# Feed-forward of an encoder layer on one core: stationary tiles in other addresses, a tanh one place later, three stretches in another order

## The chip, the cores and the metric

The kernel runs on one core of a Trainium2 chip. The metric is the device time of one execution in microseconds, less is better. PE is TensorE, DVE is VectorE, ACT is ScalarE, POOL is GpSimd and SP is SyncE, whose queue issues nearly all transfers.

## The reference

The part that matters is the last third of the layer, for 2048 tokens, width 1024 and a hidden width of 2816. All arithmetic is float32.

```python
hff = rms_norm(x, g_norm2) * (1.0 + scale2) + shift2
gte, up = jnp.split(hff @ w_ffn_in, 2, axis=-1)
ff = (jax.nn.silu(gte) * up) @ w_ffn_out
x = x + gate2 * ff            # then rms_norm(x, g_final)
```

## The kernel before, in words

**Arithmetic.** A float32 operand is split into a high and a low part (ACT copies the high part, DVE subtracts to get the low one), and each product is three matmuls: high by high, high by low, low by high (`mm3`, lines 56 to 58). Both large products of the feed-forward are done blockwise with seven block products in place of eight (A11, A12, S4, A22, S1, S2, S3), so that sums and differences of blocks have to be made on POOL and DVE.

**First product, units.** `pair(hh, j, ...)` is one unit: half `hh` of the tokens, block `j` of the hidden columns. It runs seven products on PE, `prod(0)` to `prod(6)`, of 12 matmuls each (four blocks of K, three matmuls each), 84 in all. The weights of a unit are the stationary operand, the activations (`hop`, seven operands of 128x4x512) the moving one. Products 0, 2, 4 and 6 add on in one PSUM bank (`ps1`): each waits until the sum before it has been copied out, by ACT in lines 1564 (`s1`), 1572 (`u2`) and 1578 (`u3`). Product 5 adds on in `ps5`, which ACT copies out in line 1575 (`c5`). Two tanh stand in a unit: line 1568 on `g0`, which DVE makes in line 1567 from product 1, and line 1583 on `u2`. Results are stored to DRAM (`a_d`) by `stores()`, at the head of the next unit. There are 44 units: 22 for the first half of the tokens, 22 for the second.

**Weights.** `load_raw` fetches the weights of a unit (three transfers, `graw`, `A21`, `A22r`), and `weights` makes the seven split tiles from them, in steps that `beside` hands out between the products of the unit before (`STEPS`). The split tiles come from a ring of 12 slots of 4 KB: `big28` to `big31`, the four tiles of pool `w`, and `r0` to `r3` in pool `ff`.

**The turn.** Unit 21 is the last of the first half of the tokens. There `refill_ops(1)` loads the seven `hop` operands of the second half in their old places, operand u as soon as product u of unit 21 is done (`start`), in two pieces of 512 KB each, and `finish_op` splits them on ACT and DVE (lines 1371, 1372). Units 21 and 22 use the same weights. The splits of operands 5 and 6 stand between the first products of unit 22.

**Second product, passes.** Seven passes (A11, S2, S3, A22, S1, S4, A12) go over 11 steps of K each. A step takes one stationary pair (`ah`, `al`, from `raw_a` and `split_a`) and one weight tile `w2`, 24 matmuls in eight PSUM banks. The stationary pairs come from a ring of four (`aring`): two pairs in `r0` to `r3`, two in pool `w`. The `w2` tiles lie in the four `xt` tiles of pool `xp`.

**Addresses.** Pools on the left side start at 0 and those on the right hang down from 224 KB of each partition. In the feed-forward the left side holds constants up to 5 KB, the 32 tiles of `big` up to 133 KB, pool `w` up to 155 KB and pool `xp` from there (its four `xt` from 155 to 171 KB). On the right is `ff`, 184 to 224 KB, with `r0` to `r3` at 200 to 216 KB.

**Order.** PE follows the program's order throughout. DVE, ACT, POOL and SP follow the order written in the program (a manual schedule, `rest`) up to `rest.close()`, which stands after the last unit. What is written behind it is put in order by the scheduler, which may also place it among the instructions of the region.

Of the kernel before, what the change touches and what calls it, by code (L numbers as in the profile page):

```python
# [21 lines left out]
P = 128  # L22
T = 2048
D = 1024
# [12 lines left out]
def hybrid_layer_kernel(  # L37
# [1276 lines left out]
    def norm2(hh, z, tags, lead):  # L1314
        n = BO[2 * hh + z]
        xt = [xp.tile([P, D], F32, tag="xt", name="x1t", bufs=4) for _ in range(4)]
# [42 lines left out]
    def refill_ops(hh):  # L1359
# [9 lines left out]
        def finish(u):  # L1369
            for hi, lo in zip(*hls[u]):  # L1370
# [6 lines left out]
                 + [("ff", f"r{i}") for i in range(4)])  # L1377
# [7 lines left out]
    def load_raw(j, early=False):  # L1385
# [4 lines left out]
        a22 = (xd.tile([P, 512], F32, tag="n2", name="A22r", bufs=9) if early else  # L1390
               pools["ff"].tile([P, 512], F32, tag="tm", name="A22r", bufs=2))
        cg, cu = (slice(o + j * P, o + (j + 1) * P) for o in (0, DFF))
        sp.dma_start(v(g), w_ffn_in[:, cg].rearrange("(k p) c -> p k c", p=P))
        sp.dma_start(v(a21), w_ffn_in[0:512, cu].rearrange("(k p) c -> p k c", p=P))
        sp.dma_start(v(a22), w_ffn_in[512:1024, cu].rearrange("(k p) c -> p k c", p=P))
        return g, a21, a22
# [38 lines left out]
    for p in range(NPR):  # L1435
# [4 lines left out]
        if p == NPR - 1:  # L1440
            hop, finish_op, refill = refill_ops(0)

            def after(u):
                if u == 6:
                    raws.append(load_raw(KH, True))
                refill(u)
                if u > 2:
                    finish_op(u - 3)
            first_w = weights(first_raw, True)
        fill.append(out_proj(cur, xr0, after))  # L1450
        for i in range(28):
# [12 lines left out]
            if i == 8 and p == NPR - 2:  # L1464
                first_raw = load_raw(0, True)
# [62 lines left out]
    with tc.tile_pool(name="ff", bufs=1, side="right", reuse_waits="tile") as ff:  # L1528
# [15 lines left out]
        def pair(hh, j, ws_, hop, after=lambda u: None, then=lambda u: None):  # L1544
# [23 lines left out]
            act.activation(t0, g0, AF.Tanh, scale=0.5)  # L1568
            dve.scalar_tensor_tensor(g0, t0, 1.0, g0, ADD, MUL)
            then(1)  # L1570
            prod(2, ps1)
            act.activation(u2, ps1, AF.Copy)  # L1572
            then(2)
# [45 lines left out]
        raw, = raws  # L1619
        for n, (hh, j) in enumerate(units[:-1]):  # L1620
# [5 lines left out]
            else:  # L1626
                more_w = weights(raw)
            STEPS = (0, 0, 0, 2, 2, 1, 2) if n == 0 else (0, 0, 1, 1, 2, 2, 1)

            def beside(u):  # L1630

                nonlocal nxt_w, raw
# [4 lines left out]
                if turn:  # L1637
                    if u > 1:
                        finish_op(u - 2)
                    return  # L1640
                for _ in range(STEPS[u]):
                    nxt_w = next(more_w)
                if u == 6 and wseq:
# [9 lines left out]
        aring = deque([("ff", f"r{i}") for i in range(4)] + [("w", f"w{i}{z}") for i in (1, 0) for z in "hl"])  # L1653
        wring = deque([("xp", "xt")] * 4)
# [73 lines left out]
        def operands(u, k):  # L1728
            if u == "A11":
                load_w2(W11, k)  # L1730
            if u == "S2":
                load_w2(W22, k)
            a = load_a(u, k)
            w = op_w(u, k)
            if u == "A11" :
                load_w2(W12, k)
            return a, w

        g2h = wp.tile([P, D], F32, tag="wraw", name="g2h", bufs=1)
        early, raw_ = [], []  # L1740

        def first_operands(u):

            if u < 2:
                raw_.append(raw_a("A11", u))
            if u == 2:
                sp.dma_start(g2h, gate_d[1].partition_broadcast(P))
            if u in (2, 4):
                early.append((split_a(*raw_[u // 2 - 1]), op_w("A11", u // 2 - 1)))
            if u in (3, 5):  # L1750
                load_w2(W12, u // 2 - 1)
            if u == 5:
                pool.tensor_scalar(g2h, g2h, 0.5, None, MUL)

        for k in range(2):
# [3 lines left out]
        rest.close()  # L1759
# [57 lines left out]
        def evac(u, i, ps):  # L1817
            if u == "A11":
                ra.append(big(16 + i, "ra", (P, D), F32))
            if u == "S3":  # L1820
                rb.append(big(24 + i, "rb", (P, D), F32))
# [21 lines left out]
        for u in ("A11", "S2", "S3", "A22", "S1", "S4", "A12"):  # L1843
# [56 lines left out]
```

## Time and profile before

| | |
|---|---|
| median of 3 runs | 2343.58 us (2342.69 to 2345.49) |
| the profiled execution | 2334.39 us |
| its span, first to last instruction | 2332.6 us |
| PE busy | 2247.8 us, 96% of the span, 10822 matmuls |
| DVE, ACT, POOL busy | 1609.4, 1062.4, 1047.1 us |
| mean granted clock of PE | 0.991 |
| units (first product) | 1013.9 to 1890.4 us of the span |
| passes (second product) | 1890.4 to 2324.4 us |

A row of the timeline is the start in the span, the duration, the engine, the line of the program, the operation with its tiles, and in brackets how long the engine had been idle and what ended that. Matmuls overlap in the pipeline, so a matmul's duration (0.39 us) is longer than the distance from one start to the next, and it is the distance that counts. A row that ends in x2 is two instructions one after the other.

### The profile page before, as it was taken

The page shows a single profiled execution, that of the slowest core. Times are in us where ns is not written, and L with a number is a line of the kernel's source. Part 1 is how long each engine was busy: PE and PEld are TensorE (multiplying, and loading weights), DVE is VectorE, ACT ScalarE, POOL GpSimd, SP SyncE. Part 2 cuts the span into 40 slices and gives each one's busy share as a digit, 9 for nine tenths or more (in the row PEclk, how much of TensorE's full clock was granted, in tenths as well). Part 3 has the DMA queues.
Part 4 walks back from the last instruction along what each step waited for, and adds up shares of the span by engine and source line. Part 5 has one row for each costly group of instructions (what it writes and reads, how often), then busy time and mean ns, then how long its engine had stood idle before and what let it go on. Part 6 is the DMA issues. An engine that isn't in the chain of part 4 may idle for free.

```text
span 2332.6 us, 32476 instructions
## 1 busy us (share of the span) xinstructions
PE 2247.8 (96%) x10822; PEld 1862.1 (80%) x10822; DVE 1609.4 (69%) x2995; ACT 1062.4 (46%) x2206; POOL 1047.1 (45%) x876
## 2 busy tenths in 40 slices
PE   7999989999999999999999999899999979999998
PEld 4997778888888878778888887688888868888887
DVE  6786667767687887786666776666666635685594
ACT  5424555544577756354444434333333323232352
POOL 1007534334334344536565655556565652592020
PEclk9999999999999999999999999999999999999999
DMA  8486755676766576764343445223232373543462
GB/s 331 150 256 218 241 155 163 176 215 188 200 176 191 169 245 218 256 221 144 109 167 104 162 159 201 83 95 109 95 108 95 127 261 100 159 153 100 136 217 90
DMA packets 355499, 393.38 MB, mean 169 GB/s; under 512 B 21388, under 2 KB 253180, under 8 KB 355332
## 3 DMA queue, kind: packets, MB, share of 16 engines
q1 hardware_dynamic: 355108, 391.28, 52.2%
q8 instruction: 85, 1.39, 0.2%
q14 instruction: 82, 0.67, 0.1%
q10 hardware_dynamic: 224, 0.04, 0.0%
HBM read 272.05 MB, written 119.19 MB: 168 GB/s over the span
## 4 chain that ended last, share of the span: by engine, by line
PE 54%; DVE 1%; DMA 1%; issue 1%; ACT 1%; POOL 0%; SPq 0%; DVEq 0%; ACTq 0%; POOLq 0%
PE fp L56 12%; PE fp L58 12%; PE fp L57 12%; PE fo L58 6%; PE fo L56 6%; PE fo L57 6%; PE ops L56 1%; DMA al<-a_d 1%; PE ops L58 1%; PE ops L57 1%; DMA B<-hop_d 0%; PE trn L166 0%; DVE B L1372 0%; DVE T L1372 0%; DMA T<-hop_d 0%
## 5 line engine op out<-in xcount | busy, mean ns | idle before, releaser
L466 PE MATMUL gps<-hT,whi 128*128 128x512 f32 x1088 | 397.3, 419 | 0.2 <-DVE cacc L500 0.2
L56 PE MATMUL fo<-w,ah 128*128 128x512 f32 x616 | 242.3, 393 | 5.0 <-ACT ah L1667 2.3
L58 PE MATMUL fo<-w,al 128*128 128x512 f32 x616 | 242.4, 393 | 1.2 <-DVE al L1668 1.2
L57 PE MATMUL fo<-w,ah 128*128 128x512 f32 x616 | 242.1, 393 | 0.0
L466 PE MATMUL gps<-hT,wlo 128*128 128x512 f32 x544 | 228.3, 420 | 0.0
L466 PEld LDWEIGHTS gps<-hT,whi 128*128 128x128 f32 x1088 | 201.9, 191 | 24.6 <-DVE cacc L500 0.6
L56 PE MATMUL fp<-T,S 128*128 128x512 f32 x528 | 208.9, 396 | 9.3 <-ACT u L1572 8.4
L57 PE MATMUL fp<-T,S 128*128 128x512 f32 x528 | 207.5, 393 | 0.0
L58 PE MATMUL fp<-T,S 128*128 128x512 f32 x528 | 207.4, 393 | 0.0
L1668 DVE TENSOR_TENSOR al<-al,ah 128x1024 fp32r<-128x1024 f32 x77 | 114.5, 1490 | 131.7 <-ACT ah L1667 131.6
L1407 DVE TENSOR_TENSOR A<-graw,A 128x512 fp32r<-128x512 f32 x86 | 105.2, 1227 | 113.7 <-ACT A L1406 113.5
L1667 ACT ACTIVATE ah<-al 128x1024 fp32r<-128x1024 f32 x77 | 81.5, 1060 | 201.2 <-DMA al<-a_d 193.7
L1407 DVE TENSOR_TENSOR S<-sf,S 128x512 fp32r<-128x512 f32 x86 | 128.8, 1535 | 61.5 <-ACT S L1406 61.4
L56 PEld LDWEIGHTS fo<-w,ah 128*128 128x128 f32 x616 | 116.0, 188 | 32.8 <-ACT ah L1667 2.8
L58 PEld LDWEIGHTS fo<-w,al 128*128 128x128 f32 x616 | 115.9, 188 | 27.8 <-DVE al L1668 1.6
L56 PE MATMUL fp<-B,A 128*128 128x512 f32 x352 | 137.6, 391 | 0.0
L58 PE MATMUL fp<-B,A 128*128 128x512 f32 x352 | 137.6, 391 | 0.0
L57 PE MATMUL fp<-B,A 128*128 128x512 f32 x352 | 137.6, 391 | 0.0
L57 PEld LDWEIGHTS fo<-w,ah 128*128 128x128 f32 x616 | 115.9, 188 | 26.1
L758 POOL TENSOR_SCALAR ap<-ap,adn 128x384 f32<-128x384 f32 (+1 forms) x128 | 73.3, 594 | 124.7 <-DVE adn L756 48.7
L56 PEld LDWEIGHTS fp<-T,S 128*128 128x128 f32 x528 | 99.6, 189 | 32.5 <-ACT u L1572 9.2
L1411 POOL TENSOR_TENSOR sf<-A,A22r 128x512 f32<-128x512 f32 x43 | 58.1, 1352 | 142.5 <-DMA A22r<-in_w_ffn_in_dram 109.6
(419 smaller groups left out, 6137.5 us busy)
## 6 DMA issues: line engine op xcount, KB each, us to landing
al<-a_d SPq DMA_DIRECT2D x77, 512.0 KB, 3.8
wmod<-in_w_mod_dram SPq DMA_DIRECT2D x48, 512.0 KB, 7.3
graw<-in_w_ffn_in_dram SPq DMA_DIRECT2D x43, 512.0 KB, 3.9
a_d<-ka SPq DMA_DIRECT2D x66, 256.0 KB, 4.7
bc<-bc_d SPq DMA_DIRECT2D x64, 256.0 KB, 3.9
hop_d<-n SPq DMA_DIRECT2D x56, 256.0 KB, 4.3
a_d<-u SPq DMA_DIRECT2D x55, 256.0 KB, 4.6
mqk<-qk_d SPq DMA_DIRECT2D x48, 256.0 KB, 4.2
```

Source lines behind the costliest of these rows:

```text
L56: pe.matmul(o, lh, rh, start=first, stop=False, skip_group_check=skip)
L57: pe.matmul(o, lh, rl, start=False, stop=False, skip_group_check=skip)
L58: pe.matmul(o, ll, rh, start=False, stop=last, skip_group_check=skip)
L466: pe.matmul(ps, w[i == 2][:, k, :], hT[n](i == 1, k), start=(k == 0 and i == 0), stop=(k == KT - 1 and i == 2))
L758: pool.tensor_scalar(self.p[g][:, :self.NK], self.p[g][:, :self.NK], dn[:, g:g + 1], 0.0, MUL, ADD)
L1407: dve.tensor_tensor(t[:, 1, :], f, t[:, 0, :].bitcast(F32), SUB)
L1411: pool.tensor_tensor(f1, a21, a22, ADD)
L1667: act.activation(ah, al.bitcast(F32), AF.Copy)
L1668: dve.tensor_tensor(al, al.bitcast(F32), ah.bitcast(F32), SUB)
```

## The change

The ring of 12 weight slots and the ring of stationary pairs take `r0` to `r3` from pool `xp` in place of `ff`, and the four `xt` rows of `norm2`, which PE transposes, move to `ff` in exchange. So `r0` to `r3` lie at 155 to 171 KB and `xt` at 200 to 216 KB. The `w2` tiles of the passes move to `big28` to `big31`. Four of the eight result rows `rb` go to `xt` in `ff`. In the last pass the pairs added to the ring are other `big` tiles and two of `xt`.

In a unit, the first tanh and the multiplication behind it are written after the copy of `u2` in place of before `prod(2)`.

At the turn, the weights that are fetched at the end of unit 20 are fetched after product 0 of unit 22, and their split steps begin at product 3 of that unit. The `A22r` of the second unit's weights is loaded at the head of the feed-forward rather than before the last operand of the first half.

In the last unit and the first pass, the loads and splits of the first pass are written out by hand between the products of the last unit and between the steps of the pass, and `rest.close()` moves to the end of pass A11. The ring of pairs starts with the tiles of pool `w`.

```diff
-        xt = [xp.tile([P, D], F32, tag="xt", name="x1t", bufs=4) for _ in range(4)]
+        xt = [pools["ff"].tile([P, D], F32, tag="xt", name="x1t", bufs=4) for _ in range(4)]
...
-                 + [("ff", f"r{i}") for i in range(4)])
+                 + [("xp", f"r{i}") for i in range(4)])
...
-        sp.dma_start(v(a22), w_ffn_in[512:1024, cu].rearrange("(k p) c -> p k c", p=P))
-        return g, a21, a22
+        return (g, a21) if "ff" not in pools and j else (g, a21, load_a22(j))
...
             dve.tensor_tensor(g0, ps2, s1_, ADD)
-            act.activation(t0, g0, AF.Tanh, scale=0.5)
-            dve.scalar_tensor_tensor(g0, t0, 1.0, g0, ADD, MUL)
             then(1)
             prod(2, ps1)
             act.activation(u2, ps1, AF.Copy)
+            act.activation(t0, g0, AF.Tanh, scale=0.5)
+            dve.scalar_tensor_tensor(g0, t0, 1.0, g0, ADD, MUL)
...
-        raw, = raws
+        raw, more_w = (*raws[0], load_a22(KH)), None
...
-            STEPS = (0, 0, 0, 2, 2, 1, 2) if n == 0 else (0, 0, 1, 1, 2, 2, 1)
+            STEPS = (0, 0, 0, 2, 2, 1, 2) if n in (0, NJ) else (0, 0, 1, 1, 2, 2, 1)
...
+                if u == 1:
+                    more_w = weights(raw)
                 for _ in range(STEPS[u]):
                     nxt_w = next(more_w)
-                if u == 6 and wseq:
+                if wseq and (u == 6 and n != NJ - 2 or u == 0 and n == NJ):
                     raw = load_raw(wseq.popleft())
...
-        aring = deque([("ff", f"r{i}") for i in range(4)] + [("w", f"w{i}{z}") for i in (1, 0) for z in "hl"])
-        wring = deque([("xp", "xt")] * 4)
+        aring = deque([("w", f"w{i}{z}") for i in (1, 0) for z in "hl"] + [("xp", f"r{i}") for i in range(4)])
+        wring = deque([("big", f"big{i}") for i in (29, 30, 31, 28)])
...
+        def split_early():
+            k = next(todo_)
+            early.append((split_a(*raw_[k]), op_w("A11", k)))
+
+        def first_operands(u):
+
+            if u in (1, 3, 5):
+                raw_.append(raw_a("A11", len(raw_)))
+            for k in ((2, 3), range(4, 8), range(8, KH))[u] if u < 3 else ():
                 load_w2(W11, k)
...
+            if u in (2, 4, 6):
+                split_early()
+            if u in (4, 5):
+                load_w2(W12, u - 4)
+            if u == 6:
                 sp.dma_start(g2h, gate_d[1].partition_broadcast(P))
...
+        raw_.append(raw_a("A11", 0))
         for k in range(2):
             load_w2(W11, k)
         pair(1, JO[0], nxt_w, hop, then=first_operands)
         stores()
-        rest.close()
+        pool.tensor_scalar(g2h, g2h, 0.5, None, MUL)
...
-                rb.append(big(24 + i, "rb", (P, D), F32))
+                rb.append(big(24 + i, "rb", (P, D), F32) if i < 4 else ff.tile([P, D], F32, tag="xt", name="rb", bufs=4))
...
+                if u == "A11":
+                    if k and k + 3 < KH:
+                        raw_.append(raw_a("A11", k + 3))
+                    if k + 2 < KH:
+                        load_w2(W12, k + 2)
+                    for k_ in (k,) if k < 8 else range(8, KH):
+                        load_w2(W22, k_)
+                    if k:
+                        split_early()
...
-                aring.extendleft(("big", f"big{31 - i}") for i in range(8))
-            tail = [operands(u, k) for k in range(KH - KL, KH)]
+                aring.extendleft([("ff", "xt")] * 2 + [("big", f"big{i}") for i in (1, 0, 27, 26, 25, 24)])
+            if u == "A11":
+                rest.close()
+            tail = [early.pop(0) if early else operands(u, k) for k in range(KH - KL, KH)]
```

## Rows read from the trace of the kernel before

**Rows 1.** Waits of PE from 1010 us on: total, times, longest.

```profile
PE fp L56 <- ACT u L1572: 8.4, 2, 8.0
PE fp L56 <- ACT c L1575: 7.4, 3, 5.7
```

**Rows 2.** Timeline of PE: first matmuls of units 24, 25, 26, of pass S2's steps 0, 1, 2.

```profile
1498.15 0.39 PE L56 MATMUL fp<-B,A 128*128 128x512 f32 x1
...
1517.51 0.39 PE L56 MATMUL fp<-B,A 128*128 128x512 f32 x1
...
1536.55 0.39 PE L56 MATMUL fp<-B,A 128*128 128x512 f32 x1
...
1960.11 0.39 PE L56 MATMUL fo<-w,ah 128*128 128x512 f32 x1
...
1965.55 0.39 PE L56 MATMUL fo<-w,ah 128*128 128x512 f32 x1
...
1971.15 0.39 PE L56 MATMUL fo<-w,ah 128*128 128x512 f32 x1
```

**Rows 3.** Timeline of PE: first matmuls of units 21, 22 (product 4 too), 23, 43, of passes A11, S3.

```profile
1426.73 0.39 PE L56 MATMUL fp<-B,A 128*128 128x512 f32 x1
...
1447.51 0.40 PE L56 MATMUL fp<-B,A 128*128 128x512 f32 x1
...
1467.81 0.79 PE L56 MATMUL fp<-T,S 128*128 128x512 f32 x1 [7.96 <-ACT u L1572]
...
1478.96 0.39 PE L56 MATMUL fp<-B,A 128*128 128x512 f32 x1
...
1863.45 0.39 PE L56 MATMUL fp<-B,A 128*128 128x512 f32 x1
...
1890.41 0.39 PE L56 MATMUL fo<-w,ah 128*128 128x512 f32 x1
...
2020.90 0.39 PE L56 MATMUL fo<-w,ah 128*128 128x512 f32 x1
```

**Rows 4.** Busy time by stretch: window, length, engines' busy us (instructions), PE's clock, DMA, GB/s.

```profile
1467.80:1473.00 5.20, 5.19 (x12) 4.12 (x13) 2.21 (x3) 1.49 (x3) 0.00 (x0) 0.50 0.00 0
```

**Rows 5.** Timeline of ACT in unit 22, the first tanh.

```profile
1464.76 0.63 ACT L1568 ACTIVATE t<-g 128x512 f32<-128x512 f32 x1 [8.79 <-DVE g L1567]
```

**Rows 6.** Timeline of DVE in unit 22.

```profile
1455.78 3.94 DVE L1372 TENSOR_TENSOR T<-T,T 128x1024 fp32r<-128x1024 f32 x2
1459.64 4.48 DVE L1372 TENSOR_TENSOR B<-B,B 128x1024 fp32r<-128x1024 f32 x2
1464.04 0.68 DVE L1567 TENSOR_TENSOR g<-fp,s 128x512 f32<-128x512 f32 x1
...
1466.36 2.36 DVE L1372 TENSOR_TENSOR T<-T,T 128x1024 fp32r<-128x1024 f32 x2 [0.25 <-ACT T L1371]
```

**Rows 7.** Timeline of SP's queue at the turn.

```profile
1430.09 0.38 SPq L1393 DMA_DIRECT2D graw<-in_w_ffn_in_dram  x1
...
1432.98 2.92 SPq L1367 DMA_DIRECT2D B<-hop_d  x4
...
1458.66 0.32 SPq L1541 DMA_DIRECT2D a_d<-u  x1
```

**Rows 8.** Timeline of SP's queue and of ACT in the last unit.

```profile
1874.69 0.33 SPq L1663 DMA_DIRECT2D al<-a_d  x1
...
1881.06 1.06 ACT L1667 ACTIVATE ah<-al 128x1024 fp32r<-128x1024 f32 x1 [3.35 <-DMA al<-a_d]
...
1882.54 0.58 ACT L1575 ACTIVATE c<-fp 128x512 f32<-128x512 f32 x1
```

**Rows 9.** Timeline of POOL, SP's queue and ACT in pass A11.

```profile
1909.77 1.29 POOL L1609 TENSOR_TENSOR ka<-ka,g 128x512 f32<-128x512 f32 x1
...
1911.52 0.36 SPq L1663 DMA_DIRECT2D al<-a_d  x1
...
1917.11 1.06 ACT L1667 ACTIVATE ah<-al 128x1024 fp32r<-128x1024 f32 x1 [11.39 <-DMA al<-a_d]
```

More of the change, by code (lines that the diff above doesn't have):

```diff
@@ L1383, in ring_tile, with load_raw @@
         return pools[pl].tile(list(shape), F32R, tag=tag, name=name, bufs=1)
-    def load_raw(j, early=False):
+    def load_raw(j):
         v = lambda t: t.rearrange("p (k c) -> p k c", c=P)
@@ L1389, in load_raw @@
         a21 = wp.tile([P, 512], F32, tag="oth", name="A21", bufs=1)
-        a22 = (xd.tile([P, 512], F32, tag="n2", name="A22r", bufs=9) if early else
-               pools["ff"].tile([P, 512], F32, tag="tm", name="A22r", bufs=2))
         cg, cu = (slice(o + j * P, o + (j + 1) * P) for o in (0, DFF))
@@ L1394, in load_raw, with load_a22 @@
         sp.dma_start(v(a21), w_ffn_in[0:512, cu].rearrange("(k p) c -> p k c", p=P))
-        sp.dma_start(v(a22), w_ffn_in[512:1024, cu].rearrange("(k p) c -> p k c", p=P))
-        return g, a21, a22
+        return (g, a21) if "ff" not in pools and j else (g, a21, load_a22(j))
+    def load_a22(j):
+        a22 = (pools["ff"].tile([P, 512], F32, tag="tm", name="A22r", bufs=2) if "ff" in pools else
+               xd.tile([P, 512], F32, tag="n2", name="A22r", bufs=9))
+        sp.dma_start(a22.rearrange("p (k c) -> p k c", c=P),
+                     w_ffn_in[512:1024, DFF + j * P:DFF + (j + 1) * P].rearrange("(k p) c -> p k c", p=P))
+        return a22
     def weights(raw, early=False):
@@ L1444, in after @@
                 if u == 6:
-                    raws.append(load_raw(KH, True))
+                    raws.append(load_raw(KH))
                 refill(u)
@@ L1464, in hybrid_layer_kernel @@
             if i == 8 and p == NPR - 2:
-                first_raw = load_raw(0, True)
+                first_raw = load_raw(0)
             pull(1)
@@ L1625, in hybrid_layer_kernel @@
                 assert not norms
-            else:
-                more_w = weights(raw)
-            STEPS = (0, 0, 0, 2, 2, 1, 2) if n == 0 else (0, 0, 1, 1, 2, 2, 1)
+            STEPS = (0, 0, 0, 2, 2, 1, 2) if n in (0, NJ) else (0, 0, 1, 1, 2, 2, 1)
             def beside(u):
-                nonlocal nxt_w, raw
+                nonlocal nxt_w, raw, more_w
                 if n == 0 and u < 3:
@@ L1728, in operands @@
         def operands(u, k):
-            if u == "A11":
-                load_w2(W11, k)
[L1731 to L1746, printed above, removed]
-                sp.dma_start(g2h, gate_d[1].partition_broadcast(P))
[L1748 to L1753, printed above, removed]
+            return load_a(u, k), op_w(u, k)
+        g2h = wp.tile([P, D], F32, tag="wraw", name="g2h", bufs=1)
+        early, raw_, todo_ = [], [], iter(range(KH))
+        def split_early():
[5 more added lines that the diff above has]
+            for k in ((2, 3), range(4, 8), range(8, KH))[u] if u < 3 else ():
+                load_w2(W11, k)
+            if u in (2, 4, 6):
[3 more added lines that the diff above has]
+            if u == 6:
+                sp.dma_start(g2h, gate_d[1].partition_broadcast(P))
+        raw_.append(raw_a("A11", 0))
         for k in range(2):
```

## The prediction

> **What bounds the kernel now.** I read the page first: PE is busy for 96% of the span, at a granted clock of 0.991. So time can only come from PE: less time per matmul, or fewer waits. The view of PE's waits from 1010 us on, where the feed-forward lies, came next: the two largest entries, 8.4 and 7.4 us, consist almost wholly of one wait each, 8.0 and 5.7 us [rows 1]. Both releasers are copies by ACT out of a bank on which PE wants to add on. The timeline of PE then gives the cost of whole stretches, by the starts of their first matmuls, which holds waits, slow clock and everything else.
>
> Matmuls first. Unit 25 takes 19.04 us, unit 24 19.36 us [rows 2]. Neither has a wait. Counting the ring of 12 from its first set (units 21 and 22 share one), unit 24 has four of its seven weight tiles in r0 to r3 and unit 25 none. So a product of 12 matmuls on such a tile costs 0.08 us more. In pass S2 step 0 takes 5.44 us and step 1 5.60 us [rows 2]; step 0's pair lies in pool w, step 1's in r0 and r1. That is 0.16 us per 24 matmuls, the same 6.7 ns per matmul, and the moving operand has not moved. The slow stationary tiles lie at 200 to 216 KB, the fast ones below 155 KB.
>
> Then the stretches. Units 21 and 22 together take 52.23 us [rows 3]; clean they would take 2 x (19.04 + 2 x 0.08) = 38.4. The turn loses 13.8 us. Unit 43 takes 26.96 us to the first matmul of the passes [rows 3], clean 19.36: 7.6 us lost. Pass A11 takes 69.70 us (from 1890.41 to S2's start at 1960.11), pass S2 60.79 us [rows 2, 3]: 8.9 us lost. Some of this is clock: after the wait of 7.96 us PE ran at half its clock, 1.2 GHz, for 12 matmuls in 5.2 us [rows 4], where the full clock takes 2.7 us (a seventh of unit 25).
>
> **The change part by part.** *Addresses.* The 43 weight sets take 301 tiles from the ring, 25 rounds and one tile, so 100 tiles in r0 to r3; the shared set holds two of them and is used twice: 102 products at 0.08 us, 8.2 us. Of the 77 pairs of the passes 73 come from the ring of four pairs, every other two in r0 to r3, which makes 37 steps at 0.16 us, hence 5.9 us. Together 14.1 us. The one step that will use two of xt in the last pass keeps its 0.2 us. The transposed rows move up: 64 transposes of 128 columns, even at a whole 6.7 ns each 0.4 us, and I take half. I count **13.7 us**. What no row shows is a stationary operand at 155 to 171 KB; it adjoins the fast region, 29 KB below the slow one, and as moving operand the w2 tiles in those very places give fast steps. Bounds 0 and 14.1; I take the fast end.
>
> On this the Trainium skill, page "SBUF — State Buffer", section "Who interferes with whom", would say otherwise: it says that PE and ACT never wait for another engine's access, and nothing in it makes one address slower than another. By it this part would give nothing. The trace disagrees, with 5.60 against 5.44 us for equal steps.
>
> *Tanh.* At the turn, ACT holds the tanh of line 1568 from 1455.97 on until DVE has made g at 1464.72, idle for 8.79 us, and the copy u2, which PE waits for [rows 3], stands behind it [rows 5]. DVE is late with g because the splits of operands 4 and 5 stand ahead [rows 6]. In the new order u2 needs product 2 alone. PE could start product 4 when product 3 was over, at 1467.81 - 7.96 = 1459.85 [rows 3], and the split of operand 4 is then just done (1459.72 [rows 6]). What is late next is DVE: operand 5 is split at 1464.12 [rows 6]. Product 4 takes 2.7 us at full clock, to 1462.6; product 5 waits to 1464.1 and ends at 1466.8. Operand 6 follows g on DVE: 1464.1 + 0.6 + 2.4 = 1467.1 [rows 6], and product 6 ends at 1469.8. Unit 22 ended at 1478.96: **9.1 us** gained, and the clock should not fall in waits of 1.5 us. In ordinary units the tanh hides as before: its g is used only after product 6, so this costs nothing there; moved in front of it in ACT is one copy of 0.58 us. In unit 0 the other wait for u2, 8.4 - 8.0 = **0.4 us** [rows 1], goes too.
>
> *Weights at the turn.* Before, three transfers of 1 MB in all stand ahead of the operands' loads in SP's queue [rows 7]. Taking them out doesn't issue the operands earlier by much, since stores of unit 20 stand between them, but it frees the transfer engines: it should save the rest of the waits in units 21 and 22 in part. The waits for c5 besides the longest come to 1.7 us [rows 1]; I take +1.0, bounds 0 and 4.7 (13.8 - 9.1). Against that, the fetch now stands behind unit 21's stores, which ended at 1458.66 [rows 7]. A transfer in a busy stretch took 6.4 us from issue to use [rows 8], so the weights are there at some 1465, POOL needs four pieces of 1.3 us each [rows 9], and the last splits come around 1471 to 1474. Behind these on ACT is the s1 copy of unit 23, for which product 2 of that unit waits, at 1469.8 + 5.4 = 1475.2. This just fits; 1.5 us is my price, bounds 0 and 5 (all of a 6.4 us landing, less what fits). Sum of the turn: **8.6 us**.
>
> *Last unit.* Before, copies for the first pass stand in ACT's order ahead of c5, and the second waits for a transfer issued at 1874.69, when product 3 was through with its tile [rows 8]. PE loses 5.7 us and the clock. Now the first pair's tiles are those of pool w that unit 42 used, free at 1863.5, so it lands by 1870 with the same 6.4 us; the second's are free after product 1. Their copies stand behind u2 and u3, at some 1872 and 1877, and find their data. **7.6 us**, bounds 4 and 7.6.
>
> *First pass.* Before, the load for step 4 goes at 1911.52, behind the last unit's stores, the last of which waits for POOL's piece of 1909.77; ACT gets its data at 1917.11 [rows 9]. POOL was late because scheduled pieces for S2 stood among its own. In the new order this queueing stays: SP still has the five stores ahead of the load for step 4. At the turn the same stores were out 11.2 us after their unit's end (1458.66 [rows 7] against unit 22's start at 1447.51 [rows 3]). So they are out at 1882.8 + 11.2 = 1894; the load lands by 1902 with the two others ahead of it, its splits (ACT 1.06, DVE 1.2 to 2) end near 1905, and step 4 is due at 1882.8 + 4 x 5.44 = 1904.6. I keep 1.5 us of loss: **7.4 us**, bounds 2 and 8.9. From step 5 on each load has two steps, 10.9 us, and needs about nine.
>
> **Sum.** 13.7 + 0.4 + 8.6 + 7.6 + 7.4 = 37.7 us. The profiled execution took 2334.39 us and would take 2296.7; the median of the runs, 9.2 us above it, goes from 2343.6 to **2305.9**. The lesser changes I cost at nothing: w2 tiles, result rows and the last pass's ring keep their number of tiles, each free a pass ahead; the second unit's A22r, now loaded at the feed-forward's head, is used from product 3 of unit 0 on, 8 us later (3 x 2.7), against 6.4 us for a landing; without that cover the wait would be under 2 us.
>
> **The rivals.** A difference under 0.2%, 4.7 us, is about what a measurement of this kernel can't tell from none.
>
> - *The tiles are slow at 155 to 171 KB too.* The address part gives nothing, 2319.6. For it: no stationary operand was seen there. Against: the neighbouring 149 to 155 KB are fast. Chance 0.08. The Trainium skill's page "SBUF — State Buffer" ("Who interferes with whom") leads to this time as well.
> - *The weights of unit 23 come late.* The turn gives back 5 to 7 us more, in waits of unit 23's first products: 2312. For it: the fetch stands behind five stores. Against: its first two splits need no POOL. Chance 0.13.
> - *The stores hold up the first pass.* SP waits for POOL with loads behind; if POOL is slowed by DVE, step 4 and perhaps step 5 wait 5 us each: 2312 to 2316. Chance 0.12.
> - *The hand-written order makes the first pass slower than it was.* Each load for step k+3 may only go when step k-1 is over. If load and splits took longer than the 10.9 us of two steps, each of the seven steps 4 to 10 would wait for the difference. To eat the whole gain takes 37.7 / 7 = 5.4 us a step, a landing and split of over 16 us; I see some nine. With the whole pass half as long again: 2350. Chance 0.03.
> - *Nothing measurable*, gains and new waits equal: 0.02.
>
> **How the numbers follow.** My forecast has 0.62, with a range of its own from 2299 (every loss named gone, 44.4 us) to 2311. The two rivals at 2312 to 2316 have 0.25 and the address rival 0.08. From 2298 to 2320 the range holds all of these but the tails, and leaves out the last two cases and surprises in the six later passes, whose order the scheduler makes anew. Faster 0.95, same 0.02, slower 0.03.
>
> **What would show it.** Right: units and steps all at 19.04 and 5.44 us; no idle PE over 2 us at the turn; ACT's u2 ahead of the tanh; c5 of unit 43 right behind product 3; clock at 1.00 after 1100 us. Wrong: units of two lengths again (addresses); a wait of PE for weights in unit 23; a wait for ah in step 4; or new waits between passes.

## The result and the profile after

The changed kernel took 2305.93 us, the kernel before 2343.14 us on the same chip (medians of four runs each): a ratio of 0.985, 95% interval 0.983 to 0.987. The forecast was 2305.9. A second set, five rounds, gave 2300.21 against 2334.74 us, again 0.985 (0.983 to 0.987).

The profiled execution has a span of 2302.1 us and a granted clock of 0.994. Of its 30.5 us less than before, 4.8 are missing because the code ahead of the feed-forward, which is the same but for one transfer, happened to take that much longer (unit 0 starts at 1018.7 us instead of 1013.9; in the eight other profiles with the same code up to there at 1014.5 to 1018.8). From the start of unit 0 to the last matmul of the passes the two profiles differ by 35.2 us, in the second set's profile by 37.2. Both are added up from the starts of first matmuls, as in the prediction:

| stretch | before, us | after | gain | second profile's gain | predicted |
|---|---|---|---|---|---|
| units 0 and 1 | 39.88 | 40.19 | −0.3 | −0.7 | 0.7 (0.4 and addresses 0.3) |
| units 2 to 20, 24 to 42 | 738.19 | 731.52 | 6.7 | 6.7 | 7.0 (addresses) |
| turn, units 21 to 23 | 71.43 | 61.60 | 9.8 | 10.3 | 9.1 (8.6 and addresses 0.5) |
| unit 43 | 26.95 | 19.04 | 7.9 | 7.9 | 7.9 (7.6 and addresses 0.3) |
| pass A11 | 69.70 | 62.20 | 7.5 | 8.3 | 8.2 (7.4 and addresses 0.8) |
| the six later passes | 364.11 | 360.50 | 3.6 | 4.7 | 5.1 (addresses) |
| sum | 1310.27 | 1275.05 | 35.2 | 37.2 | 38.0 |

(The predicted column spreads the address term over the stretches by its 102 products and 37 steps. It leaves out the 0.4 us that the prediction takes off for one step and the transposes, so its sum is 38.0 and not 37.7.)

How far two profiles of one stretch differ is to be kept in mind below. Runs whose code in a stretch is that of the changed kernel have it at 39.7 to 40.8 us (units 0 and 1), 60.3 to 61.6 (the turn) and 61.1 to 62.2 (pass A11; 63.8 in one profile in which the clock fell there). So a difference of a microsecond or less in one of these stretches says little. In the six later passes one loss is new: pass S3 takes 61.30 us (60.16 in the second profile) where the others take 59.84, and before it had 60.69 like its neighbours. It is 1.5 and 0.3 us, the prediction did not have it, and its cause stays open.

Waits of PE of the changed kernel from 1010 us on: total, times, longest. They answer to [rows 1].

```profile
PE fp L56 <- ACT s L1568: 2.9, 3, 1.2
PE fp L56 <- ACT c L1579: 2.1, 2, 1.3
PE fo L57 <- DVE w L1681: 1.9, 1, 1.9
PE fo L58 <- DVE al L1672: 0.8, 2, 0.5
```

The two waits of 8.0 and 5.7 us are gone, nothing longer than 1.9 us is left, and all that is left comes to 7.7 us. The granted clock is 1.00 from 1018 to 1871 us. Then the timeline of PE of the changed kernel: starts of units 22 to 26 and 43, of passes A11 and S2 (with S2's steps 1 and 2), and the two longest waits. It answers to [rows 2, 3].

```profile
1447.73 0.39 PE L56 MATMUL fp<-B,A 128*128 128x512 f32 x1
...
1464.23 0.50 PE L56 MATMUL fp<-B,S 128*128 128x512 f32 x1 [1.27 <-ACT c L1579]
...
1469.80 0.39 PE L56 MATMUL fp<-B,A 128*128 128x512 f32 x1
...
1490.27 0.39 PE L56 MATMUL fp<-B,A 128*128 128x512 f32 x1
...
1509.31 0.39 PE L56 MATMUL fp<-B,A 128*128 128x512 f32 x1
...
1528.35 0.39 PE L56 MATMUL fp<-B,A 128*128 128x512 f32 x1
...
1852.03 0.39 PE L56 MATMUL fp<-B,A 128*128 128x512 f32 x1
...
1871.07 0.39 PE L56 MATMUL fo<-w,ah 128*128 128x512 f32 x1
...
1895.24 0.50 PE L57 MATMUL fo<-w,ah 128*128 128x512 f32 x1 [1.92 <-DVE w L1681]
...
1933.27 0.39 PE L56 MATMUL fo<-w,ah 128*128 128x512 f32 x1
...
1938.70 0.39 PE L56 MATMUL fo<-w,ah 128*128 128x512 f32 x1
...
1944.14 0.39 PE L56 MATMUL fo<-w,ah 128*128 128x512 f32 x1
```

Units 24 and 25 now both take 19.04 us, and S2's steps 0 and 1 both 5.44: the two lengths of [rows 2] have become one. Unit 22 takes 22.07 us instead of 31.45, unit 23 takes 20.47, 1.4 more than it should.

### The profile page after: what moved, and what is told of

Read it like the earlier page. It is cut to its first block, busy times and chain, and to the rows that moved or that the text cites. A ratio compares the mean times of both kernels' runs of the same rounds, so it can differ in the third digit from the quotient of the medians.

```text
span 2302.1 us, 32525 instructions
## 1 busy us (share of the span) xinstructions
PE 2230.1 (97%) x10822; PEld 1859.8 (81%) x10822; DVE 1635.1 (71%) x2995; ACT 1061.6 (46%) x2206; POOL 1057.7 (46%) x876
## 4 chain that ended last, share of the span: by engine, by line
PE 51%; DVE 3%; DMA 2%; issue 1%; ACT 1%; POOL 0%; SPq 0%; ACTq 0%; POOLq 0%; DVEq 0%
PE fp L56 12%; PE fp L57 12%; PE fp L58 11%; PE fo L58 5%; PE fo L57 5%; PE fo L56 5%; DMA al<-a_d 1%; PE ops L56 1%; PE ops L57 1%; PE ops L58 1%; DVE al L1672 1%; DVE ra L1811 0%; DVE w L1681 0%; PE trn L166 0%; DMA T<-hop_d 0%
## 5 line engine op out<-in xcount | busy, mean ns | idle before, releaser
L1672 DVE TENSOR_TENSOR al<-al,ah 128x1024 fp32r<-128x1024 f32 x77 | 120.4, 1568 | 111.0 <-ACT ah L1671 110.9
L1411 DVE TENSOR_TENSOR A<-graw,A 128x512 fp32r<-128x512 f32 x86 | 130.2, 1536 | 16.1 <-ACT A L1410 16.0
L1576 DVE SCALAR_TENSOR_TENSOR g<-t,g 128x512 f32<-128x512 f32 x44 | 44.0, 1000 | 131.0 <-ACT t L1575 131.0
```

The source lines that it names most:

```text
L1411: dve.tensor_tensor(t[:, 1, :], f, t[:, 0, :].bitcast(F32), SUB)
L1672: dve.tensor_tensor(al, al.bitcast(F32), ah.bitcast(F32), SUB)
```

## The experiments

Four runs undo one part each, side by side (before: 2338.01 us, median of seven runs). One more takes a part of the turn apart, five move tiles, and one takes away the waits that remain, beside the changed kernel itself.

### The addresses put back

```diff
-        xt = [pools["ff"].tile([P, D], F32, tag="xt", name="x1t", bufs=4) for _ in range(4)]
+        xt = [xp.tile([P, D], F32, tag="xt", name="x1t", bufs=4) for _ in range(4)]
...
-                 + [("xp", f"r{i}") for i in range(4)])
+                 + [("ff", f"r{i}") for i in range(4)])
...
-        wring = deque([("big", f"big{i}") for i in (29, 30, 31, 28)])
+        wring = deque([("xp", "xt")] * 4)
...
-                rb.append(big(24 + i, "rb", (P, D), F32) if i < 4 else ff.tile([P, D], F32, tag="xt", name="rb", bufs=4))
+                rb.append(big(24 + i, "rb", (P, D), F32))
...
-                aring.extendleft([("ff", "xt")] * 2 + [("big", f"big{i}") for i in (1, 0, 27, 26, 25, 24)])
+                aring.extendleft(("big", f"big{31 - i}") for i in range(8))
```

> The changed kernel with its address part alone undone: r0 to r3 at 200 to 216 KB again, xt in pool xp, w2 tiles in xt, result rows and the last pass's ring as before. Theory (a stationary operand that lies there costs 6 to 7 ns per matmul): 13 to 14 us slower than the changed kernel, about 2319; units of 19.04 to 19.36 us in turn, steps of 5.44 and 5.60 us. Rival (equal addresses, the gain came from the orders): within 2 us of the changed kernel, all units 19.04 us.

Measured: 2312.23 us, ratio 0.989 (0.987 to 0.991), against 0.985 for the whole change: about 9.6 us of 2338. The expectation was 13 to 14. In this run's built program `r0` to `r3` lie at 204 to 220 KB. The stretch from unit 0 to the end is 1286.09 us, 11.0 more than in the changed kernel's first profile (1275.05) and 13.1 more than in its second (1273.04). The 38 undisturbed units take 738.17 us, what they took before within 0.02 and 6.7 more than after; unit 43 has 19.36. The later passes but S3 take 0.7 to 1.0 us more each, 4.1 in sum. The turn (61.03 us) and pass A11 (61.96) are not clearly longer: what the prediction has for the tiles there, 0.5 and 0.8, is no more than these stretches differ from profile to profile. So the term is real: 11 to 13 us of the 13.7 forecast.

### The tanh put back

```diff
             prod(1, ps2, True)
             dve.tensor_tensor(g0, ps2, s1_, ADD)
+            act.activation(t0, g0, AF.Tanh, scale=0.5)
+            dve.scalar_tensor_tensor(g0, t0, 1.0, g0, ADD, MUL)
             then(1)
             prod(2, ps1)
             act.activation(u2, ps1, AF.Copy)
-            act.activation(t0, g0, AF.Tanh, scale=0.5)
-            dve.scalar_tensor_tensor(g0, t0, 1.0, g0, ADD, MUL)
```

> The changed kernel with the first tanh back before product 2. Theory (ACT holds the copy u2 behind a tanh that waits for DVE's g): units 21 to 23 take 68 to 71 us in place of 61.6, PE waits 6 to 9 us for u2 in unit 22, 7 to 10 us slower in all, about 2314. Rival (the turn got shorter since the fetch of weights moved): units 21 to 23 within 2 us of 61.6.

Measured: 2307.09 us, ratio 0.987 (0.985 to 0.988). The times alone hardly part this from the whole change (0.985, 0.983 to 0.987); the trace does. The turn takes 67.67 us instead of 61.60: **6.1 us**, not 9.1, and just under the 68 to 71 expected. The timeline of PE and of ACT of this run, at product 4 of unit 22:

```profile
1466.51 0.80 PE L56 MATMUL fp<-T,S 128*128 128x512 f32 x1 [5.83 <-ACT u L1576]
...
1463.45 0.63 ACT L1572 ACTIVATE t<-g 128x512 f32<-128x512 f32 x1 [6.66 <-DVE g L1571]
1463.99 1.99 ACT L1371 ACTIVATE T<-T 128x1024 fp32r<-128x1024 f32 x2
1465.88 0.58 ACT L1576 ACTIVATE u<-fp 128x512 f32<-128x512 f32 x1
```

This is the mechanism of [rows 3, 5]: ACT stands idle before the tanh until DVE has made g, and u2, which needs only product 2, is behind it (and behind the two copies of operand 6, which stand ahead of u2 in the new order too). The windows view of the same run shows what follows the wait (window, length, busy us of PE, PEld, DVE, ACT and POOL with instructions, PE's clock, DMA, GB/s):

```profile
1466.50:1471.80 5.30, 5.29 (x13) 4.18 (x14) 4.21 (x3) 1.48 (x3) 5.22 (x3) 0.50 0.00 0
```

The granted clock is 0.50, 1.2 GHz, as in [rows 4]: 12 matmuls take 5.3 us there in place of 2.7, so of the 6.1 us some 2.6 are that.

### The fetch of the weights put back

```diff
-            STEPS = (0, 0, 0, 2, 2, 1, 2) if n in (0, NJ) else (0, 0, 1, 1, 2, 2, 1)
+            STEPS = (0, 0, 0, 2, 2, 1, 2) if n == 0 else (0, 0, 1, 1, 2, 2, 1)
...
-                if wseq and (u == 6 and n != NJ - 2 or u == 0 and n == NJ):
+                if u == 6 and wseq:
```

> The changed kernel with the weights at the turn fetched at unit 20's end again and split from product 2 on. Theory of the prediction (early weights save the wait of unit 23, 1.4 us, and put 1 MB ahead of the operands): within 2 us of the changed kernel. Rival 1 (POOL's pieces for the weights then run beside DVE's splits of operands 5 and 6, which take 4.5 us a pair against 2.35): the turn 3 to 5 us longer. Rival 2 (the fetch was what cost the turn): 8 us or more.

Measured: 2303.65 us, ratio 0.986 (0.984 to 0.987), too near the whole change's 0.985 to tell by the time; the trace tells it. Units 21 and 22 take 45.63 us instead of 41.13, unit 23 19.04 instead of 20.47: the late fetch gives 4.5 us and costs 1.4, **3.1 us** net, where −0.5 was forecast. The timeline of POOL, DVE, ACT and PE of this run, in unit 22:

```profile
1455.01 2.26 POOL L1415 TENSOR_TENSOR sf<-A,A22r 128x512 f32<-128x512 f32 x1
...
1456.05 4.52 DVE L1372 TENSOR_TENSOR B<-B,B 128x1024 fp32r<-128x1024 f32 x2
1460.50 0.68 DVE L1571 TENSOR_TENSOR g<-fp,s 128x512 f32<-128x512 f32 x1
...
1461.27 0.63 ACT L1575 ACTIVATE t<-g 128x512 f32<-128x512 f32 x1 [6.27 <-DVE g L1571]
1461.81 0.61 ACT L1410 ACTIVATE A<-graw 128x512 fp32r<-128x512 f32 x1
1462.33 0.58 ACT L1579 ACTIVATE c<-fp 128x512 f32<-128x512 f32 x1
...
1462.96 0.50 PE L56 MATMUL fp<-B,S 128*128 128x512 f32 x1 [3.96 <-ACT c L1579]
```

And the same place in the changed kernel, timeline of POOL, DVE and ACT:

```profile
1466.58 1.61 POOL L1415 TENSOR_TENSOR sf<-A,A22r 128x512 f32<-128x512 f32 x1 [7.56 <-DMA A22r<-in_w_ffn_in_dram]
...
1460.02 2.35 DVE L1372 TENSOR_TENSOR B<-B,B 128x1024 fp32r<-128x1024 f32 x2
1462.30 0.68 DVE L1571 TENSOR_TENSOR g<-fp,s 128x512 f32<-128x512 f32 x1
...
1463.06 0.63 ACT L1575 ACTIVATE t<-g 128x512 f32<-128x512 f32 x1 [4.33 <-DVE g L1571]
1463.59 0.58 ACT L1579 ACTIVATE c<-fp 128x512 f32<-128x512 f32 x1
...
1475.34 0.62 ACT L1410 ACTIVATE A<-A22r 128x512 fp32r<-128x512 f32 x1
1475.86 0.58 ACT L1568 ACTIVATE s<-fp 128x512 f32<-128x512 f32 x1
```

With POOL at work on the weights, DVE's two splits of operand 5 take 4.52 us (before: 4.48 [rows 6]); with POOL idle, 2.35. So g comes 2.2 us later in the early fetch, and behind g in ACT's order stand the tanh, the first copy of the new weights (0.61 us) and then c5, for which product 5 waits: 3.96 us in place of 1.27. The rest of the 4.5 is mostly the clock: it was 0.50 from 1464.2 to 1467.6 us, so that products 5 and 6 take 7.2 us in place of 5.6, while in the changed kernel it stays at 1.00. The price is in the last two rows: unit 23's s1 stands behind the late weights' last split on ACT and comes at 1475.9, when product 2 is already due (1469.80 + 2 x 2.72 = 1475.2). The Trainium skill ("SBUF — State Buffer", "Who interferes with whom") says that a VectorE instruction with two inputs in SBUF contends with a GpSimd instruction that reads SBUF; the trace agrees, at 4.52 against 2.35 us.

### Transfers or POOL

Here the weights are fetched early, as before, but their split steps begin behind product 4 and not behind product 2, so POOL's pieces, and the copies and subtractions that stand in the same steps, come after operand 5.

```diff
-            STEPS = (0, 0, 0, 2, 2, 1, 2) if n in (0, NJ) else (0, 0, 1, 1, 2, 2, 1)
+            STEPS = (0, 0, 0, 2, 2, 1, 2) if n == 0 else (0, 0, 0, 0, 3, 2, 2) if n == NJ else (0, 0, 1, 1, 2, 2, 1)
...
-                if wseq and (u == 6 and n != NJ - 2 or u == 0 and n == NJ):
+                if u == 6 and wseq:
```

> The changed kernel with the weights at the turn fetched early, at unit 20's end, but split only from product 4 of unit 22 on, so that POOL's four pieces come behind the copy of product 4 and not beside DVE's splits of operands 5 and 6. Theory (POOL beside DVE made the turn of the early fetch 3.1 us longer): units 21 and 22 some 41 us again in place of 45.6, operands 5 and 6 split in 2.4 us a pair. Rival (the early fetch itself, 1 MB ahead of the operands, costs it): units 21 and 22 stay at 44 us or more.

Measured, one run: 2297.91 us (before 2335.72). Units 21 and 22 take 41.84 us, against 41.13 after and 45.63 with the early steps. The timeline of DVE, the splits of operand 5:

```profile
1457.18 2.35 DVE L1372 TENSOR_TENSOR B<-B,B 128x1024 fp32r<-128x1024 f32 x2
```

They take 2.35 us though the transfers are early, so it is POOL's work that slows them, and of the 4.5 us 3.8 go with the split steps. The 0.7 left lies in unit 21 (19.73 us against 19.06). That the earlier transfers cost it is not shown: with the early steps unit 21 took 19.32, and in the version without the remaining waits, whose fetch is late, 19.97. A single run doesn't tell this version's time from that of the changed kernel.

### The order of last unit and first pass put back

The functions of the first pass's loads and splits, the ring's order and `rest.close()` are those of before; the rest is as after.

```diff
-        aring = deque([("w", f"w{i}{z}") for i in (1, 0) for z in "hl"] + [("xp", f"r{i}") for i in range(4)])
+        aring = deque([("xp", f"r{i}") for i in range(4)] + [("w", f"w{i}{z}") for i in (1, 0) for z in "hl"])
...
-            if u in (2, 4, 6):
-                split_early()
+            if u in (2, 4):
+                early.append((split_a(*raw_[u // 2 - 1]), op_w("A11", u // 2 - 1)))
...
         stores()
-        pool.tensor_scalar(g2h, g2h, 0.5, None, MUL)
+        rest.close()
...
```

> The changed kernel with the last unit and the first pass ordered as before: region closed after the last unit, loads and splits of the first pass left to the scheduler. Theory: unit 43 some 26.9 us in place of 19.04, pass A11 some 68 to 69 us in place of 62.2: 13 to 15 us slower, about 2320. Rival (the ring that begins in pool w, or the faster tiles, gave it): under 5 us.

Measured: 2312.97 us, ratio 0.989 (0.988 to 0.991), 10.5 us over the whole change, where 13 to 15 were expected. Unit 43 takes 27.11 us instead of 19.04, pass A11 66.81 instead of 62.20: 12.7 us in the two. The timeline of ACT and PE of this run, at product 5 of unit 43:

```profile
1864.14 1.06 ACT L1671 ACTIVATE ah<-al 128x1024 fp32r<-128x1024 f32 x1 [3.60 <-DMA al<-a_d]
...
1865.62 0.58 ACT L1579 ACTIVATE c<-fp 128x512 f32<-128x512 f32 x1
...
1866.25 0.80 PE L56 MATMUL fp<-B,S 128*128 128x512 f32 x1 [5.36 <-ACT c L1579]
```

It is [rows 8] again: the copy c5 behind a split whose data are still under way. In pass A11 the starts of the steps say more than the forecast did: before, steps 0, 3 and 4 took 8.83, 7.94 and 8.72 us, with this order 8.23, 7.40 and 7.65, after 5.44, 5.44 and 7.80. The forecast worked out one cause of the old pass's loss, at step 4, which is the one that stayed; the gain came at steps 0 and 3.

### What makes a tile slow: five more places

All of these leave the rest as it is. First `r0` to `r3` on the left, at 167 to 183 KB (other tiles of pool `xp` are placed below them).

```diff
+        for _ in range(5):
+            xp.tile([P, 512], F32, tag="n2", name="n2", bufs=5)
+        xp.tile([P, D], BF16, tag="junk", name="junk", bufs=1)
```

> The changed kernel with r0 to r3 higher in pool xp: r0 at 167 to 171 KB, r1 171 to 175, r2 175 to 179, r3 179 to 183 KB, nothing else changed. Theory (the address decides, with a border at 176 KB as the change's words have it): products on r0 and r1 take 2.72 us, on r3 2.80 us, on r2 some 2.78 to 2.80, its blocks below 176 KB at 227 ns a matmul and those above at 234. Rival 1 (the slow tiles are those of the upper pool, for what works around them there): all four 2.72 us. Rival 2 (the border lies above 183 KB): all four 2.72 us, the same; then only a higher ladder tells.

Then the moving operand: the `w2` tiles of the passes on the right, in `xt` of pool `ff`. In the built program that is 208 to 224 KB, not 200 to 216 as the section on the change says.

```diff
-        wring = deque([("big", f"big{i}") for i in (29, 30, 31, 28)])
+        wring = deque([("ff", "xt")] * 4)
...
```

> The changed kernel with the w2 tiles, the moving operand of the passes, at 208 to 224 KB, and all stationary pairs low; result rows and the last pass's ring as in the kernel before. Theory A (only the stationary operand matters): steps 5.44 us throughout. Theory B (any operand of a matmul): every step on such a tile 5.60 us or more, the six later passes 5 to 10 us longer in sum than the 360.5 of the changed kernel.

Then `r0` to `r3` on the right, but at the bottom of pool `ff`, at 184 to 200 KB (on top of the run with the addresses put back).

```diff
+        for i in range(4):
+            ff.tile([P, 4, P * 2], F32R, tag=f"r{i}", name="r", bufs=1)
```

> The address change alone undone, as in the run with the tiles back at 200 to 216 KB, but now r0 to r3 lie at 184, 188, 192 and 196 KB, so the four tiles of 4 KB are a ladder between the last place seen fast (183 KB) and the first seen slow (200 KB). Read from it is the distance from one matmul to the next for each 512-byte block of each tile, 227 ns if fast, 234 ns if slow. Theory 'a border inside that gap': the blocks below it show 227, those above it 234, with one step; at 192 KB, r0 and r1 are fast, r2 and r3 slow, and the six later passes take 60.2 to 60.3 us each. Theory 'it begins at 200 KB': all blocks 227 ns, passes of 59.84 us. Theory 'it is not the address, but the pool on the right-hand side or what its other tiles do at the same time': all blocks 234 ns, passes of 60.7 us.

The timeline of PE at unit 24: its start, its fourth product (the first of the four in r0 to r3), and unit 25's start. First with the tiles at 167 to 183 KB, left:

```profile
1488.72 0.39 PE L56 MATMUL fp<-B,A 128*128 128x512 f32 x1
...
1496.88 0.39 PE L56 MATMUL fp<-T,S 128*128 128x512 f32 x1
...
1507.76 0.39 PE L56 MATMUL fp<-B,A 128*128 128x512 f32 x1
```

And with the tiles at 184 to 200 KB, right:

```profile
1492.73 0.39 PE L56 MATMUL fp<-B,A 128*128 128x512 f32 x1
...
1500.90 0.39 PE L56 MATMUL fp<-T,S 128*128 128x512 f32 x1
...
1512.09 0.39 PE L56 MATMUL fp<-B,A 128*128 128x512 f32 x1
```

The four products take 10.88 us (2.72 each) in the first, 11.19 (2.80) in the second, all four tiles alike: of the borders in the expectations, neither the one at 176 KB nor one between 184 and 200 KB is there. The moving operand costs the same: with w2 on the right five of the six later passes take 61.60 us instead of 59.84, so (61.60 − 59.84) / 264 = 6.7 ns per matmul. (One run each: 2300.24 and 2309.71 us for the first two, before 2335.72; 2313.28 for the third, before 2334.74. The lengths of products and passes carry the argument, not these times.) A border could still lie at 183 to 184 KB. A tile on the right but below that decides it, from the output projection (a version with three waits moved, told below, with this in addition):

```diff
+    for i in range(2):
+        mx.tile([P, 2, 512], F32R, tag=f"m{i}", name="m", bufs=1)
     mring = deque([(mx, "m0"), (mx, "m1")] + [(wp, f"w{i}{z}") for i in (1, 0) for z in "hl"]
```

> As the version with three waits taken away, and, in the output projection of the attention (a stretch that the change does not touch), the two weight tiles m0 and m1 moved from 211 to 219 KB down to 175 to 183 KB, with the tiles of VectorE and the rows of x above them. Theory 'address': about 250 matmuls with these stationary tiles go from 234 to 227 ns and 1.5 to 1.8 us come off. Theory 'these tiles were slow for something else' (they are used by another loop, with another moving operand): no change against the version without it.

Measured: 2300.61 us, against 2301.34 for the version without it, no difference. In the projection the mean distance between starts is 233.2 ns for the 128 matmuls with m0 or m1 as stationary tile and 228.4 for 474 others, as in the changed kernel (233.3 and 228.5). So **height is not the cause**: 175 to 183 KB on the right is slow, 167 to 183 KB on the left fast.

What is left was in the built programs: pools on the right hang from 32 bytes below 224 KB, so the tiles there that PE reads start 32 bytes off a multiple of 64; those on the left start on multiples of 512. The last run turns this round. It pads `ff` and pool `w` by 32 bytes each (and `xp`, to stay on multiples of 64), on top of the run with the addresses put back.

```diff
+                    wp.tile([P, 8], F32, tag="pad", name="pad", bufs=1)
...
-        r = rsqrt(xp, ssq, 4, D, "rs")
+        r = rsqrt(xp, ssq, 4, D, "rs", bufs=1)
...
+    xp.tile([P, 8], F32, tag="pad", name="pad", bufs=1)
...
+        ff.tile([P, 8], F32, tag="pad", name="pad", bufs=1)
         gfb = [ff.tile([P, 512], F32, tag="sf", name="gfb", bufs=2) for _ in range(2)]
```

> The layout with the address part undone, with 32 bytes of padding in two places: r0 to r3, still on the right-hand side, move down by 32 bytes to 204 to 220 KB and lie there on multiples of 64 bytes; the four tiles of pool w, on the left at 133 to 153 KB, move up by 32 bytes and lie 32 bytes off such a multiple. The w2 tiles and the operands stay on multiples of 64. Theory 'alignment': the two change places. Matmuls whose stationary tile is one of r0 to r3 take 227 ns from start to start, those with a tile of pool w 233 to 234, in the feed-forward and, for pool w, in the output projection too, where these were fast. Theory 'height in the partition or right-hand side': as in the run with the tiles back on the right, r0 to r3 take 233 to 234 ns and pool w 227.

The timeline of PE of this run: unit 24 (three products with tiles of pool w, then four with r0 to r3) and unit 25 (four with tiles of big, then three of pool w), with the start of unit 26.

```profile
1500.30 0.40 PE L56 MATMUL fp<-B,A 128*128 128x512 f32 x1
...
1508.70 0.40 PE L56 MATMUL fp<-T,S 128*128 128x512 f32 x1
...
1519.70 0.40 PE L56 MATMUL fp<-B,A 128*128 128x512 f32 x1
...
1530.61 0.39 PE L56 MATMUL fp<-T,S 128*128 128x512 f32 x1
...
1539.00 0.40 PE L56 MATMUL fp<-B,A 128*128 128x512 f32 x1
```

Against the run with the tiles at 184 to 200 KB, right, three products on pool w go from 8.17 us to 8.40 and, in unit 25, 8.39 (2.80 each): the fast tiles at 133 to 153 KB have become slow by 32 bytes. Four products on r0 to r3 go from 11.19 to 11.00 (2.75 each): most of the way, but not to 2.72. Those tiles now start on multiples of 64, yet 64 bytes off a multiple of 128. So the start address in the partition sets the price, in grades; "64 is enough" is too simple, and whether 128 is enough no run tells. The run took 2326.89 us (before 2339.12), slower than with the addresses put back. From unit 0 on it is 8.4 us longer: 3.3 in the six passes (368.06 us against 364.73), 2.8 in the 38 undisturbed units, 1.9 in the turn. In the passes the w2 tiles, the moving operand, start 64 bytes off a multiple of 128 too. With a stationary tile that does the same, matmuls there start every 232.3 ns; with one of pool w every 233.4, hardly more than its 233.2 with an aligned moving operand. So the two prices do not simply add up.

### A version without the remaining waits

Operand 6's splits go behind product 3 in units 0 and 22, and the last unit's stores go to SP behind the load for step 5.

```diff
-                if n == 0 and u < 3:
-                    finish_op(u + 4)
-                if n == NJ and u < 2:
-                    finish_op(u + 5)
+                if n == 0 and u in (0, 1, 3):
+                    finish_op((4, 5, 0, 6)[u])
+                if n == NJ and u in (1, 3):
+                    finish_op((0, 5, 0, 6)[u])
...
-        stores()
...
+                    if k == 2:
+                        stores()
```

> The changed kernel unaltered, timed beside the two versions of this group on the same chip, so that these can be compared with it. Expected ratio to the kernel before 0.983 to 0.987, as measured first.

> The changed kernel with its three remaining waits taken away. In units 0 and 22 the splits of operand 6 come behind product 3, so that the copy c5 is no longer behind them on ACT; the stores of the last unit go to SP behind the load for step 5 of pass A11 and not ahead of that for step 4. Theory 'queueing': ACT and SP were late only because of what stood ahead of them, so PE's waits at c5 (2.1 us), and at step 4 (about 2.2 us, L57 and L58) go, and 3 to 5 us come off the changed kernel (2306 becomes 2301 to 2303). Rival 'the data themselves are late': the waits move to product 6, to steps 5 and 6, or to the POOL sums that the stores free, and the time is within 1.5 us of the changed kernel.

Measured side by side: 2301.34 us, ratio 0.985 (0.984 to 0.987), against 2300.21 and 0.985 (0.983 to 0.987) for the changed kernel: no better, where 3 to 5 us were expected. (Stretches of the changed kernel are those of its profile in this set.) Pass A11 takes 59.84 us, so its loss at step 4 is gone, and SP's order was its cause. But units 0 and 1 take 42.57 us instead of 40.61, and the turn 63.68 instead of 61.11. The timeline of DVE, ACT and PE of this version, in unit 1, and a row of its windows view:

```profile
1037.45 3.48 DVE L1411 TENSOR_TENSOR S<-sf,S 128x512 fp32r<-128x512 f32 x2
...
1041.62 0.63 ACT L1587 ACTIVATE t<-u 128x512 f32<-128x512 f32 x1 [5.14 <-DVE u L1586]
...
1043.72 0.58 ACT L1568 ACTIVATE s<-fp 128x512 f32<-128x512 f32 x1
...
1044.35 0.50 PE L56 MATMUL fp<-T,S 128*128 128x512 f32 x1 [2.36 <-ACT s L1568]
...
1040.00:1050.00 10.00, 7.64 (x27) 5.81 (x26) 6.81 (x9) 3.79 (x7) 3.59 (x3) 0.83 0.35 104
```

The wait for c5 is gone and one for s1 has taken its place: DVE is late with the weights' splits, ACT's tanh waits for DVE, and s1 stands behind it. The same wait, 1.88 us, comes in unit 23. Behind both the clock is 0.50 for 3.4 us, which costs 1.7 us each time: 3.4 of the 4.5 us that the two stretches lose. The version with the two tiles of the output projection moved has the same edits here, and in its profile the waits for s1 are 1.70 and 1.52 us, the clock stays at 1.00, and units 0 and 1 take 40.07, the turn 61.42. From unit 0 to the end that profile takes 1272.05 us, the changed kernel's 1273.04 and this version's 1276.18. So with the clock at 1.00 the edits are worth 1.0 us, and with the clock's falls behind the moved waits, which came in one of the two profiles, they cost 3.1.

## Why the prediction was right, point by point

- **The number.** That the median came out at 2305.93 for a forecast of 2305.9 is luck. The second set had 2300.21; the medians gained 37.2 and 34.5 us, the traced stretches 35.2 and 37.2, for 37.7 forecast. And the terms below miss by up to 3.6 us, both ways. The causes that it named were the right ones, but for the reason given for the addresses.
- **Addresses: 13.7 forecast, 11.0 to 13.1 shown.** Per product and per step the price was right (0.076 and 0.16 us). The reason given, nearness to the fast region, was wrong: a tile on the right at 175 to 183 KB is slow and one on the left is fast. What the change altered is the start's remainder, 0 in place of 32 bytes after multiples of 64. The rows shown before could not tell these apart, for the slow tiles were at once high, on the right, and off by 32, and the bytes stand only in the built program. The new places happened to answer the same way by all three: that too was luck. The section of the Trainium skill's page "SBUF — State Buffer" that the prediction holds against the trace is about one engine's wait for another; a price by start address is no such wait, so the trace does not disagree with it.
- **Tanh: 9.1 forecast, 6.1 shown with all else in place.** The step that failed is "What is late next is DVE": the working let product 5 start as soon as operand 5 was split, and passed over c5. In the new order c5 stands on ACT behind the tanh, and the tanh behind g. With the early fetch, the case that the prediction worked out, product 5 waits 4.0 us for that and not 1.5, the clock falls, and units 21 and 22 gain 6.6 us (52.23 to 45.63), 0.3 of them by the addresses. With the late fetch the wait is 1.3.
- **Fetch: −0.5 forecast, +3.1 shown.** The term +1.0 measured 4.5, near its upper bound of 4.7: POOL's work beside DVE, which lengthens the splits from 2.35 to 4.5 us, had not been counted, nor the clock behind the longer wait. The term −1.5 measured 1.4. The errors of tanh and fetch cancel, by luck: 8.6 forecast for the two, 6.1 + 3.1 = 9.2 shown.
- **Last unit: 7.6 forecast and shown** (7.9 with the address part; 8.1 when the order alone is put back).
- **First pass: 7.4 forecast with 1.5 lost at step 4.** Lost are 2.4 (1.6 in the second profile), at that step and for that reason. The timeline of SP's queue, ACT, POOL and DVE of the changed kernel, which answers to [rows 9]:

```profile
1880.94 0.32 SPq L1545 DMA_DIRECT2D a_d<-ka  x1
...
1883.27 0.38 SPq L1667 DMA_DIRECT2D al<-a_d  x1
...
1891.19 1.06 ACT L1671 ACTIVATE ah<-al 128x1024 fp32r<-128x1024 f32 x1 [15.19 <-DMA al<-a_d]
...
1879.29 1.62 POOL L1613 TENSOR_TENSOR ka<-ka,g 128x512 f32<-128x512 f32 x1
...
1893.42 1.76 DVE L1681 TENSOR_TENSOR w<-w2x,w 128x512 fp32r<-128x512 f32 x1
```

  The store waits for POOL's last piece and the load for step 4 is queued behind it. Step 4 was due at 1871.07 + 4 x 5.44 = 1892.8, and the last of its splits ends on DVE at 1895.2.
- **Unit 0: +0.4 forecast, −0.3 and −0.7 in the two profiles.** The wait for u2, 0.40 us, went, but that for c5, 0.34 before, is 0.79 and 1.29, behind operand 6's splits on ACT, and unit 1 waits 0.7 us for s1. All of this is about the size by which the stretch differs between profiles.
- **Rivals.** Slow tiles at the new places: no. The weights of unit 23 late: 1.4 us, not 5 to 7. Stores in the way of the first pass: 2.4 us, at step 4 alone. All small enough to leave the sum standing.

## What to carry to other kernels

When tiles of one shape have two prices, list their start addresses in full, remainders too, before naming a region: here 32 bytes, not 40 KB, made the difference. A pad at the end of a pool that brings its tiles onto multiples of 512 bytes would be the first thing to try; no run here did that. When an instruction is moved in front of another on one engine, look at what comes to stand behind the one that was moved: the tanh gave u2 its freedom and took some of it from c5. And where one engine slows another, moving its work in time can be worth more than moving transfers: here 3.8 us of 4.5.

## What the runs showed of the hardware

- Matmuls of 128x128 on 128x512 in full clock start every 227 ns if both operands begin on multiples of 512 bytes, and every 233 ns if the stationary or the moving one begins 32 bytes off a multiple of 64 (means over 1,200 to 3,700 starts of a run). With the stationary one 64 bytes off a multiple of 128 it is 229 ns, with both so 232. The Trainium skill ("SBUF — State Buffer", "Operand start alignment") asks for a multiple of the element size and says that its runs timed nothing; here such starts have a price.
- Two splits on DVE of 128x1024 each, both inputs in SBUF, took 2.35 us with POOL idle and 4.5 us with POOL adding tiles at the same time.
- After a wait of 5.8 us PE's granted clock was 0.50 for the next 5.3 us, as after the 8.0 us of before. After waits of 1.9 us it did either: 0.50 for 3.4 us behind the wait of 1.88 in unit 23 of the version without the remaining waits, and at step 4 of pass A11 with the early fetch; 1.00 behind the wait of 1.92 at that same step in the changed kernel.
